# Attention scores of a two-layer hybrid block: the keys' low parts meet only the queries' high part, on half-height tiles of the array

## The chip, the cores and the metric

The kernel runs on one core of one Trainium2 chip. The metric is the device time of one execution in microseconds (us); lower is better. TensorE is called PE, its weight loads PEld, VectorE DVE, ScalarE ACT, GpSimd POOL, and SyncE, which issues most transfers, SP.

## The reference, cut to what matters

Two layers, each with three mixers side by side (an RG-LRU, an SSD scan and a differential attention), an output projection and a SwiGLU network. The change is in the scores of the attention. There are 4 heads, each with two components of 64 features; 1024 latent tokens read 1280 keys (256 context, 1024 latent), and in the first layer the 256 context tokens read the 256 context keys.

```python
def diff_attn_core(q, k, v, lam):
    s = jnp.einsum("bqhcd,bkhcd->bhcqk", q, k).astype(F32)   # c: the two components, d: 64 features
    p = jax.nn.softmax(s, axis=-1)
    w = (p[:, :, 0] - lam * p[:, :, 1]).astype(v.dtype)
    return jnp.einsum("bhqk,bkhd->bqhd", w, v)
```

## The kernel before, in words

Operands of the large products are held as two numbers in a faster matmul type (fp32r): a high part, which is the rounded value, and a low part, which is what rounding took away. A product is then a sum of a few products of parts.

In the attention the 64 features of a component fill only half of the array's 128 rows. The kernel before fills both halves: the tile `qs` holds the queries' high part on rows 0 to 63 and their low part on rows 64 to 127, and the tiles `kh` and `kl` hold the keys' high and low part twice, once on each half. A matmul of `qs` with `kh` gives both products with the keys' high part at once, and one with `kl` both products with the keys' low part, so all four products of parts are formed.

The function `prep(hd)` makes these tiles for a head: `load` brings the raw rows twice, `split_k` and `split_q` make the parts (the rounding copies on ACT, the subtractions on DVE for head 0 and on POOL for the other heads). Its steps are called one at a time, at the place marked "X" in the order of operations, while the head before is worked on.

The work on scores goes in units: one head and 128 queries, 32 latent units in each layer and 4 context units in layer 0. One pass of the loop over `s` (called a step here) does, for units of different age, the operations that the list `K["ops"]` names: "Q0" and "Q1" form the scores of the two components of a unit (the function `qk`; one component of a latent unit is called a part here), "T0" and "T1" transpose the weights of an older unit on PE (`trans`), "P0" and "P1" multiply an older pair of units with the values (`pv`), "E1" is a matmul with ones for a norm (`subln`), "W" and "C" scale and combine the two softmaxes (`weigh` on POOL, `combine` on DVE). A part's scores lie in a PSUM tile `s` of 1280 columns, three banks, of which there are two (`sps`). After the matmuls of a part DVE takes the row maxima (`m`), ACT takes the exponential (`p`), and then the PSUM tile is free for the part after the next.

The order on each engine is set by a scheduler when the kernel is built; in some stages PE follows the order in which the code is written.

Elsewhere the kernel has matmuls that use only some of the array's columns at a time, side by side: L418 (4 tiles of 128 rows by 32 columns, the modulation) and L1064 (2 tiles of 128 rows by 64 columns, in the SSD mixer).

The line numbers below are those of the kernel before: L1212 and L1213 are the score matmuls with `kh` and `kl`, L1216 the maxima, L1220 the exponential, L1249 the transposes, L1259 the products with the values, L1275 the matmul with ones, L1235 the combination, L1172 and L1173 the two operations of `split_q`, L139 and L140 those of `split`.

Of the kernel before, what the change touches and what calls it, by code (L numbers as in the profile page):

```python
# [8 lines left out]
F32 = mybir.dt.float32  # L9
F32R = mybir.dt.float32r  # L10
AF = mybir.ActivationFunctionType
ALU = mybir.AluOpType
AX = mybir.AxisListType

P = 128
# [4 lines left out]
T = NCX + NLAT  # L20
# [56 lines left out]
def kernel(ctx: ExitStack, tc: tile.TileContext, I, out):  # L77
# [3 lines left out]
    act = nc.scalar  # L81
    pool = nc.gpsimd
    pe = nc.tensor
# [7 lines left out]
    def nm(s):  # L91
        uid[0] += 1
        return f"{s}{uid[0]}"
# [17 lines left out]
    def bank(shape, tag="b"):  # L111
        if TAGS[0] is not None:
            tag = "D" if tag == "b" else tag
            return PS[0].tile(shape, F32, tag=tag, name=nm(tag), bufs=TAGS[0][tag])
        return PS[0].tile(shape, F32, tag="b", name=nm("b"))
# [11 lines left out]
    def lagged(f, key=None):  # L127
        if LAG[0] is None:
            return f()
        flush()  # L130
        LAG[0].append((f, key))
# [6 lines left out]
    def split(hi, lo, src, lo_eng=None, key=None):  # L138
        act.copy(hi, src)  # L139
        lagged(lambda: (lo_eng or dve).tensor_tensor(lo, src, hi.bitcast(F32), ALU.subtract), key)  # L140
# [593 lines left out]
    for l in range(DEPTH):  # L734
# [404 lines left out]
        def att(shape, tag, bufs=1, dt=F32, pl=None):  # L1139
            return (pl or AT[1]).tile(shape, dt, tag=tag, name=nm(tag), bufs=bufs)  # L1140
# [4 lines left out]
        def prep(hd):  # L1145

            q0 = NCX if last else 0

            eng = dve if hd == 0 else pool
            pl = AT[hd % 2]  # L1150
            D = HD[hd] = {}

            def load(c, isq):
                t0 = q0 if isq else 0
                raw = D[c, isq] = att([P, T], "raw", 2, F32, at0)
                src = (qD if isq else kD)[hd][64 * c:64 * c + 64, t0:T]
                sy.dma_start(raw[0:64, t0:T], src)
                sy.dma_start(raw[64:128, t0:T], src)

            def first():  # L1160
                for n in ("kh", "kl", "qs"):
                    D[n] = att([P, 2, T], n, 1, F32R, pl)
                load(0, False)
                load(1, False)

            def split_k(c):
                split(D["kh"][:, c, :], D["kl"][:, c, :], D[c, False], eng)
                load(c, True)

            def split_q(c):  # L1170
                raw, qs = D[c, True][:, q0:T], D["qs"][:, c, q0:T]
                act.copy(qs, raw)  # L1172
                eng.tensor_tensor(qs[64:128], raw[64:128], qs[64:128].bitcast(F32), ALU.subtract)  # L1173

            def load_v():
                D["vt"] = att([P, 10, P], "v", 1, F32, pl)
                sy.dma_start(D["vt"], vD[:, hd * P:(hd + 1) * P].rearrange("(j p) d -> p j d", p=P))

            return [first, lambda: split_k(0), lambda: split_k(1), lambda: split_q(0), lambda: split_q(1), load_v]

        units = []
# [6 lines left out]
        def nkey(qb):  # L1188
            return NCX if qb == 0 else T

        def qk(i, c, extra=None):


            hd, qb, qt = units[i]
            D = HD[hd]
            nk = nkey(qb)
            if c == 0:
                U[i] = dict(m=att([P, 4], "m", 3), l=att([P, 4], "l", 3), p=[])
            u = U[i]
            if qb == 0:  # L1200
                if c == 1:
                    return
                parts = [(t, cc, t * P) for t in range(2) for cc in range(2)]
            else:
                parts = [(qt, c, qb * 256 + qt * P)]
            n = len(parts)
            st = sps.tile([P, 1536], F32, tag="s", name=nm("s"))
            s = st[:, 0:n * nk].rearrange("p (n k) -> p n k", n=n)
            for a, (_, cc, tq) in enumerate(parts):
                for k0 in range(0, nk, 512):  # L1210
                    w = min(512, nk - k0)
                    pe.matmul(s[:, a, k0:k0 + w], D["qs"][:, cc, tq:tq + P], D["kh"][:, cc, k0:k0 + w], start=True, stop=False)  # L1212
                    pe.matmul(s[:, a, k0:k0 + w], D["qs"][:, cc, tq:tq + P], D["kl"][:, cc, k0:k0 + w], start=False, stop=True)  # L1213
            if extra is not None:
                extra(st[:, 1280:1536])
            dve.tensor_reduce(u["m"][:, c:c + n], s, AX.X, ALU.max, negate=True)  # L1216
            pt_ = {cc: att([P, n // 2 * nk if n > 1 else nk], *(("p1", 3) if cc else ("p0", 4))) for cc in {cc for _, cc, _ in parts}}
            for a, (_, cc, _) in enumerate(parts):
                p = pt_[cc][:, a // 2 * nk:(a // 2 + 1) * nk]
                act.activation(p, s[:, a, :], AF.Exp, bias=u["m"][:, c + a:c + a + 1], accum_out=u["l"][:, c + a:c + a + 1])  # L1220
                u["p"].append(p)
# [30 lines left out]
        def pv(i, part):  # L1252
            hd, qb, _ = units[i]
            nch = nkey(qb) // P
            if part == 0:
                HD["o", hd, qb] = bank([P, 256])
            op = HD["o", hd, qb]
            for j in range(nch // 2 * part, nch // 2 * (part + 1)):
                pe.matmul(op, HD[hd]["vt"][:, j, :], HD["w", hd, qb][:, j, :], start=(j == 0), stop=(j == nch - 1))  # L1259
            if part == 1:  # L1260
                o = att([P, 256], "o", 3)
                dve.tensor_copy(o, op)
                HD["o", hd, qb] = o

        def subln(i, part):
            hd, qb, _ = units[i]
            o = HD["o", hd, qb]
            if part == 0:
                sq = att([P, 256], "sq", 2)
                pool.tensor_tensor(sq, o, o, ALU.mult)  # L1270
                HD["s", hd, qb] = sq
                return
            if part == 1:
                sp_ = bank([P, 256])
                pe.matmul(sp_, ones, HD["s", hd, qb], start=True, stop=True)  # L1275
                rs = att([P, 256], "rs", 2)
                act.activation(rs, sp_, AF.Ln, scale=1.0 / P, bias=epsc)
                act.activation(rs, rs, AF.Exp, scale=-0.5)
                HD["r", hd, qb] = rs
                return  # L1280
            rs = HD["r", hd, qb]
            dve.scalar_tensor_tensor(o, o, par[l]["gs"], rs, ALU.mult, ALU.mult)
            sy.dma_start(mixD[4 + hd][:, qb * 256:(qb + 1) * 256], o)
# [29 lines left out]
        for s in range(nu + 7):  # L1313
            if s < nu and s % per == 0 and units[s][0] < 3:
                todo = prep(units[s][0] + 1)
            e0 = (lambda ps=None: trans(s - 3, 2, ps)) if isu(s - 3) and units[s - 3][1] else None
            for op in K["ops"][l]:
                if op == "L0" and second(s - 5): subln(s - 5, 0)
                if op == "T0" and isu(s - 3): trans(s - 3, 0)
                if op == "T1" and isu(s - 3): trans(s - 3, 1)  # L1320
                if op == "W" and isu(s - 1): weigh(s - 1)
                if op == "Q0" and isu(s): qk(s, 0, e0)
                if op == "Q1" and isu(s): qk(s, 1)
                if op == "C" and isu(s - 2): combine(s - 2)
                if op == "P0" and second(s - 4): pv(s - 4, 0)
                if op == "P1" and second(s - 4): pv(s - 4, 1)
                if op == "E0" and e0 and not isu(s): e0()
                if op == "E1" and second(s - 5): subln(s - 5, 1)
                if op == "L2" and second(s - 6): subln(s - 6, 2)
                if op == "X" and todo: todo.pop(0)()  # L1330
                if op in ("X", "Q1") and s < 3:
                    for _ in range(2):
                        adaln_step(ada1, None, True)
            if s == 2:
                adaln_end()
# [335 lines left out]
        for d in range(0, KD, 2):  # L1671
            for b in ob:
                s0, n = BLK[b]
# [166 lines left out]
```

## Time and profile before

| | us |
|---|---|
| median of 3 runs | 3141.62 (3140.46 to 3142.94) |
| the profiled execution, its own time | 3142.72 |
| span of the profiled execution, first to last instruction | 3140.7 |
| PE busy in the span | 3013.6 (96%) |
| DVE busy in the span | 2034.3 (65%) |
| ACT busy in the span | 1377.5 (44%) |
| POOL busy in the span | 385.2 (12%) |

The engines work at the same time, so these do not add up. The score matmuls of the attention run from 468.7 to 688 us (layer 0) and from 2106 to 2304 us (layer 1) of the span. A matmul's row in the trace gives its start and a duration that runs to the end of its results; matmuls that follow one another overlap, so how long a matmul holds the array is read from the start of one row to the start of the next.

### The profile page before, as it was taken

What the parts mean: (1) busy time and instruction counts of PE and PEld (TensorE: products, weight loads), DVE (VectorE), ACT (ScalarE), POOL (GpSimd) and SP (SyncE); (2) the same over time, 40 slices, a digit from 0 to 9 for tenths busy, and PEclk for the clock granted to TensorE, in tenths of its full rate; (3) what the DMA queues carried; (4) which work ended last, traced back from release to release, by engine and by line L of the source; (5) the groups of instructions that cost most, each with busy time, mean ns of one, the idle gap of its engine ahead of it and who ended that gap; (6) DMA issues with size and microseconds to landing.
All of it is one profiled execution on the core that took longest, in us unless ns stands there. A gap on an engine that the chain in (4) does not pass through costs nothing. (4 is left out here: it accounts for less than half of the span.)

```text
span 3140.7 us, 41892 instructions
## 1 busy us (share of the span) xinstructions
PE 3013.6 (96%) x15825; PEld 2469.6 (79%) x15825; DVE 2034.3 (65%) x3088; ACT 1377.5 (44%) x2491; POOL 385.2 (12%) x386
## 2 busy tenths in 40 slices
PE   6999998999999999999999899999989899999998
PEld 4888776788778788888888689877868688887887
DVE  5744657976764455557777764668956766666777
ACT  6643736765432323332212645746744433333122
POOL 1113114532000000000000013115421000000000
PEclk8999999999999999999999999999999999999999
DMA  9127565208234331225222224444124122225231
GB/s 310 55 78 216 172 180 140 70 14 265 73 110 134 109 123 59 82 70 200 84 81 84 83 81 126 120 132 131 36 101 150 54 81 81 82 85 195 95 94 61
DMA packets 327441, 353.11 MB, mean 112 GB/s; under 512 B 22237, under 2 KB 269382, under 8 KB 327238
## 3 DMA queue, kind: packets, MB, share of 16 engines
q1 hardware_dynamic: 327062, 350.36, 35.9%
q8 instruction: 124, 2.03, 0.3%
q14 instruction: 79, 0.65, 0.1%
q10 hardware_dynamic: 176, 0.07, 0.0%
HBM read 268.05 MB, written 82.31 MB: 112 GB/s over the span
## 5 line engine op out<-in xcount | busy, mean ns | idle before, releaser
L139 ACT CAST wo<-wr 128x512 fp32r<-128x512 f32 x374 | 230.3, 620 | 451.9 <-issue 145.2
L1467 PE MATMUL A<-x,wo 128*128 128x512 f32 x1584 | 392.4, 396 | 7.2 <-DVE wo L140 5.1
L1659 DVE SCALAR_TENSOR_TENSOR h<-b,mod,h 128x512 f32<-128x512 f32 (+1 forms) x456 | 300.9, 677 | 121.6 <-PE b L123 111.4
L140 DVE TENSOR_TENSOR wo<-wr,wo 128x512 fp32r<-128x512 f32 x374 | 253.8, 688 | 191.9 <-ACT wo L139 186.5
L1467 PEld LDWEIGHTS A<-x,wo 128*128 128x128 f32 x1584 | 294.5, 189 | 81.7 <-issue 7.6
L122 PE MATMUL b<-hl,wo 128*128 128x512 f32 (+1 forms) x912 | 333.8, 366 | 3.2 <-DVE hl L140 3.1
L121 PE MATMUL b<-hh,wo 128*128 128x512 f32 (+1 forms) x912 | 333.3, 366 | 3.6 <-ACT hh L139 3.4
L123 PE MATMUL b<-hh,wo 128*128 128x512 f32 (+1 forms) x912 | 332.4, 365 | 0.0
L121 PE MATMUL b<-xh,wh 128*128 128x512 f32 (+1 forms) x848 | 310.8, 367 | 4.0 <-ACT xh L139 4.0
L122 PE MATMUL b<-xl,wh 128*128 128x512 f32 (+1 forms) x848 | 305.4, 360 | 5.4 <-DVE xl L493 4.2
L123 PE MATMUL b<-xh,wl 128*128 128x512 f32 (+1 forms) x848 | 305.2, 360 | 0.0
L1467 PE MATMUL B<-x,wo 128*128 128x512 f32 x1056 | 263.7, 396 | 8.0 <-DVE x L140 5.5
L1467 PEld LDWEIGHTS B<-x,wo 128*128 128x128 f32 x1056 | 196.9, 189 | 57.4 <-DVE x L140 10.9
L1220 ACT ACTIVATE p<-s,m 128x1280 f32<-128x1280 f32 (+1 forms) x144 | 177.4, 1234 | 69.8 <-DVE m L1216 65.1
L121 PEld LDWEIGHTS b<-hh,wo 128*128 128x128 f32 x912 | 171.7, 189 | 35.7 <-ACT hh L139 4.9
L122 PEld LDWEIGHTS b<-hl,wo 128*128 128x128 f32 x912 | 172.4, 189 | 34.7 <-DVE hl L140 4.9
L1216 DVE TENSOR_REDUCE m<-s 128x1 f32<-128x1280 f32 (+1 forms) x132 | 190.6, 1472 | 10.8 <-PE s L1213 10.7
L123 PEld LDWEIGHTS b<-hh,wo 128*128 128x128 f32 x912 | 172.3, 189 | 28.6
L121 PEld LDWEIGHTS b<-xh,wh 128*128 128x128 f32 x848 | 163.0, 192 | 35.1 <-issue 5.5
L122 PEld LDWEIGHTS b<-xl,wh 128*128 128x128 f32 x848 | 161.7, 191 | 33.0 <-DVE xl L493 4.7
L1212 PE MATMUL s<-kh,qs 128*128 128x512 f32 (+1 forms) x400 | 157.0, 394 | 24.8 <-ACT p L1220 22.0
L123 PEld LDWEIGHTS b<-xh,wl 128*128 128x128 f32 x848 | 161.6, 191 | 23.2
(340 smaller groups left out, 5984.6 us busy)
## 6 DMA issues: line engine op xcount, KB each, us to landing
aw<-in_w_mod_dram SPq DMA_DIRECT2D x96, 512.0 KB, 4.7
wr<-in_w_in_dram SPq DMA_DIRECT2D x44, 512.0 KB, 3.9
wr<-in_w_gate_dram SPq DMA_DIRECT2D x44, 512.0 KB, 3.8
wr<-in_w_up_dram SPq DMA_DIRECT2D x44, 512.0 KB, 3.8
hid<-s SPq DMA_DIRECT2D x44, 512.0 KB, 2.6
wr<-in_w_down_dram SPq DMA_DIRECT2D x44, 512.0 KB, 3.2
t<-hid SPq DMA_DIRECT2D x88, 256.0 KB, 3.1
wr<-in_w_out_dram SPq DMA_DIRECT2D x40, 512.0 KB, 4.4
```

The costliest lines, as they stand in the source:

```text
L121: pe.matmul(o, wh, xh, start=first, stop=False)
L122: pe.matmul(o, wh, xl, start=False, stop=False)
L123: pe.matmul(o, wl, xh, start=False, stop=last)
L139: act.copy(hi, src)
L140: lagged(lambda: (lo_eng or dve).tensor_tensor(lo, src, hi.bitcast(F32), ALU.subtract), key)
L1212: pe.matmul(s[:, a, k0:k0 + w], D["qs"][:, cc, tq:tq + P], D["kh"][:, cc, k0:k0 + w], start=True, stop=False)
L1216: dve.tensor_reduce(u["m"][:, c:c + n], s, AX.X, ALU.max, negate=True)
L1220: act.activation(p, s[:, a, :], AF.Exp, bias=u["m"][:, c + a:c + a + 1], accum_out=u["l"][:, c + a:c + a + 1])
L1467: pe.matmul(o, w[x][:, k, :], r[y][:, k, :], start=first and k == 0 and i == 0, stop=k == 3 and i == 2, skip_group_check=True)
L1659: dve.scalar_tensor_tensor(hv, ps, sect(l, 5, b, d), hv, ALU.mult, ALU.add)
```

## The change

The product of the low parts (keys' low with queries' low) is no longer formed. The keys' low parts are kept once, not twice: keys 0 to 511 and 1024 to 1279 on rows 0 to 63 of a new tile `lq`, keys 512 to 1023 on its rows 64 to 127, beside a copy of the queries' high part for those rows. A part's scores are now three matmuls with `kh` over all 128 rows and then three matmuls with low parts on tiles of 64 rows: 512 keys on the upper half of the array, 512 on the lower half, 256 on the upper half. `split_k` has three subtractions over 64 rows in place of one over 128, `split_q` one more copy on ACT. To make room, three small buffers become fewer (`o` 3 to 2, `sq` and `rs` 2 to 1).

```diff
             def split_k(c):
-                split(D["kh"][:, c, :], D["kl"][:, c, :], D[c, False], eng)
+                raw, kh, lq = D[c, False], D["kh"][:, c, :], D["lq"][:, c, :]
+                act.copy(kh, raw)
+                for r, o, k0, n in ((0, 0, 0, 512), (0, 512, 1024, 256), (64, T, 512, 512)):
+                    r = slice(r, r + 64)
+                    eng.tensor_tensor(lq[r, o:o + n], raw[r, k0:k0 + n], kh[r, k0:k0 + n].bitcast(F32), ALU.subtract)
                 load(c, True)
 
             def split_q(c):
                 raw, qs = D[c, True][:, q0:T], D["qs"][:, c, q0:T]
                 act.copy(qs, raw)
+                act.copy(D["lq"][64:128, c, q0:T], raw[64:128])
                 eng.tensor_tensor(qs[64:128], raw[64:128], qs[64:128].bitcast(F32), ALU.subtract)
...
             for a, (_, cc, tq) in enumerate(parts):
+                q, lq = D["qs"][:, cc, tq:tq + P], D["lq"][:, cc, :]
                 for k0 in range(0, nk, 512):
                     w = min(512, nk - k0)
-                    pe.matmul(s[:, a, k0:k0 + w], D["qs"][:, cc, tq:tq + P], D["kh"][:, cc, k0:k0 + w], start=True, stop=False)
-                    pe.matmul(s[:, a, k0:k0 + w], D["qs"][:, cc, tq:tq + P], D["kl"][:, cc, k0:k0 + w], start=False, stop=True)
+                    pe.matmul(s[:, a, k0:k0 + w], q, D["kh"][:, cc, k0:k0 + w], start=True, stop=False)
+                pe.matmul(s[:, a, 0:min(512, nk)], q[0:64], lq[0:64, 0:min(512, nk)], start=False, stop=True, tile_position=(0, 0))
+                if nk == T:
+                    pe.matmul(s[:, a, 512:1024], lq[64:128, tq:tq + P], lq[64:128, T:T + 512], start=False, stop=True, tile_position=(64, 0))
+                    pe.matmul(s[:, a, 1024:T], q[0:64], lq[0:64, 512:768], start=False, stop=True, tile_position=(0, 0))
```

On PE, in the middle of layer 0's attention, one part (the scores `s`), the transposes after it (`b`, `s` out of `ident` and `p`) stood like this before:

```order
L1212 MATMUL s_4977<-kh_4372,qs_4374 128x512
L1213 MATMUL s_4977<-kl_4373,qs_4374 128x512
L1212 MATMUL s_4977<-kh_4372,qs_4374 128x512
L1213 MATMUL s_4977<-kl_4373,qs_4374 128x512
L1212 MATMUL s_4977<-kh_4372,qs_4374 128x256
L1213 MATMUL s_4977<-kl_4373,qs_4374 128x256
L1249 MATMUL s_4977<-ident,p_4836 128x128 x2
```

and stand like this now (lines of the changed kernel: L1218 is the matmul with `kh`, L1219, L1221 and L1222 are those on half-height tiles, L1258 the transposes, L1268 the products with the values, L1284 the matmul with ones):

```order
L1218 MATMUL s_4989<-kh_4372,qs_4373 128x512 x2
L1218 MATMUL s_4989<-kh_4372,qs_4373 128x256
L1219 MATMUL s_4989<-lq_4374,qs_4373 128x512
L1221 MATMUL s_4989<-lq_4374 128x512
L1222 MATMUL s_4989<-lq_4374,qs_4373 128x256
L1258 MATMUL s_4989<-ident,p_4847 128x128 x2
```

The six matmuls of a part stay together, but the three on half-height tiles now stand between full-height ones. In the whole order there are 153 such runs of half-height matmuls: 119 are the whole three of a part, 16 the single matmul of a context part, and 18 belong to 9 parts whose three are split by other work. Behind 65 of the 153 a transpose follows, behind 88 another full matmul (the products with the values, the matmul with ones, the next part or the modulation).

On PE a context unit (four parts of 256 keys) of layer 0 stands like this now, where before L1212 and L1213 took turns at the same place:

```order
L1218 MATMUL s_5038<-kh_4372,qs_4373 128x256
L1219 MATMUL s_5038<-lq_4374,qs_4373 128x256
L1218 MATMUL s_5038<-kh_4372,qs_4373 128x256
L1219 MATMUL s_5038<-lq_4374,qs_4373 128x256
L1218 MATMUL s_5038<-kh_4372,qs_4373 128x256
L1219 MATMUL s_5038<-lq_4374,qs_4373 128x256
L1218 MATMUL s_5038<-kh_4372,qs_4373 128x256
L1219 MATMUL s_5038<-lq_4374,qs_4373 128x256
```

Here full-height and half-height matmuls alternate one by one, four times in each of four units.

On ACT, in layer 1, where a later head is prepared, the queries' copy `lq` is new among the copies of weights (`wT`) and the exponentials (ACTIVATE):

```order
L1176 CAST qs_18533<-raw_18645 128x1024
L1259 COPY wT_18668<-b_18712 128x4x128
L1177 CAST lq_18534<-raw_18645 64x1024
L1229 ACTIVATE p_18710,l_18676<-s_18702,m_18675 128x1280
L1259 COPY wT_18668<-b_18733 128x4x128
```

Before, the exponential followed the copy of the weights without L1177; there are 16 such casts in the program, 4 of them ahead of the attention's loops.

## Rows read from the trace of the kernel before

**Rows 1.** The page: busy time, share of the span, instructions.

```profile
PE 3013.6 (96%) x15825; PEld 2469.6 (79%) x15825; DVE 2034.3 (65%) x3088; ACT 1377.5 (44%) x2491; POOL 385.2 (12%) x386
```

**Rows 2.** Busy time by stretch, ramp and steady part of each attention; after it clock, DMA.

```profile
core 0: us, PE busy (x) PEld busy (x) DVE busy (x) ACT busy (x) POOL busy (x), PEclk, DMA share, GB/s
468.00:500.00 32.00, 22.12 (x134) 14.09 (x132) 23.78 (x27) 18.31 (x22) 14.28 (x7) 0.89 0.79 213
...
520.00:688.00 168.00, 161.60 (x895) 135.81 (x894) 149.56 (x172) 125.69 (x224) 78.60 (x56) 1.00 0.18 46
...
2150.00:2304.00 154.00, 151.12 (x845) 129.89 (x844) 138.62 (x155) 114.44 (x188) 69.30 (x48) 1.00 0.18 48
```

**Rows 3.** Waits, 2150 to 2300 us: who, for whom, total, times, longest.

```profile
ACT p L1220 <- DVE m L1216: 16.3, 19, 1.4
...
PEld s L1212 <- ACT p L1220: 4.1, 6, 1.4
PE s L1212 <- ACT p L1220: 2.8, 4, 1.1
```

**Rows 4.** PE in order of time, layer 1 attention: start, length, engine, line, operation.

```profile
2227.68 2.32 PE L1259 MATMUL b<-wT,v 128*128 128x256 f32 x10
2229.84 0.60 PE L1249 MATMUL b<-ident,p 128*128 128x128 f32 x4
2230.20 0.48 PE L1212 MATMUL s<-kh,qs 128*128 128x512 f32 x1
2230.52 0.40 PE L1213 MATMUL s<-kl,qs 128*128 128x512 f32 x1
2230.75 0.40 PE L1212 MATMUL s<-kh,qs 128*128 128x512 f32 x1
...
2231.33 0.28 PE L1213 MATMUL s<-kl,qs 128*128 128x256 f32 x1
2231.45 0.38 PE L1249 MATMUL s<-ident,p 128*128 128x128 f32 x2
...
2233.36 2.32 PE L1259 MATMUL b<-wT,v 128*128 128x256 f32 x10
```

**Rows 5.** PE in order of time, SSD mixer of layer 0, around column tiles.

```profile
319.96 0.28 PE L122 MATMUL b<-xl,wh 128*128 128x256 f32 x1
320.08 0.28 PE L123 MATMUL b<-xh,wl 128*128 128x256 f32 x1
320.29 0.64 PE L418 MATMUL ada<-aw,cst 128*32 128x256 f32 x8
...
321.35 0.39 PE L1064 MATMUL b<-E,xt 128*64 128x128 f32 x4
321.57 0.39 PE L1064 MATMUL b<-CE,He 128*64 128x128 f32 x4
321.89 0.51 PE L1036 MATMUL b<-amh,gtr 128*128 128x512 f32 x1
322.23 0.39 PE L1037 MATMUL b<-aml,gtr 128*128 128x512 f32 x1
```

**Rows 6.** PE in order of time, column tiles between score matmuls, layer 0.

```profile
493.98 0.39 PE L1212 MATMUL s<-kh,qs 128*128 128x512 f32 x1
494.21 0.39 PE L1213 MATMUL s<-kl,qs 128*128 128x512 f32 x1
494.53 0.64 PE L418 MATMUL b<-aw,cst 128*32 128x256 f32 x8
495.10 0.39 PE L1212 MATMUL s<-kh,qs 128*128 128x256 f32 x1
495.32 0.28 PE L1213 MATMUL s<-kl,qs 128*128 128x256 f32 x1
```

**Rows 7.** Casts of `split_q` and subtractions for `kl`: durations ns min/median/max.

```profile
L1172 ACT CAST qs<-raw x16: 1034/1150/1263, 463.3 to 2232.0; 128x1280 fp32r<-128x1280 f32 x8, 128x1024 fp32r<-128x1024 f32 x8
...
L140 POOL TENSOR_TENSOR kl<-raw,kh x12: 2890/2928/2959, 479.2 to 2224.5; 128x1280 fp32r<-128x1280 f32 x12
```

More of the change, by code (lines that the diff above doesn't have):

```diff
@@ L1160, in first @@
             def first():
-                for n in ("kh", "kl", "qs"):
-                    D[n] = att([P, 2, T], n, 1, F32R, pl)
+                for n, w in (("kh", T), ("qs", T), ("lq", T + 512)):
+                    D[n] = att([P, 2, w], n, 1, F32R, pl)
                 load(0, False)
@@ L1260, in pv @@
             if part == 1:
-                o = att([P, 256], "o", 3)
+                o = att([P, 256], "o", 2)
                 dve.tensor_copy(o, op)
@@ L1268, in subln @@
             if part == 0:
-                sq = att([P, 256], "sq", 2)
+                sq = att([P, 256], "sq", 1)
                 pool.tensor_tensor(sq, o, o, ALU.mult)
@@ L1275, in subln @@
                 pe.matmul(sp_, ones, HD["s", hd, qb], start=True, stop=True)
-                rs = att([P, 256], "rs", 2)
+                rs = att([P, 256], "rs", 1)
                 act.activation(rs, sp_, AF.Ln, scale=1.0 / P, bias=epsc)
```

## The prediction

> **What bounds the kernel now.** I read the page first. PE is busy for 96% of the span, the next engine, DVE, for 65% [rows 1]. But the change lies in the two attentions alone, so the busy time by stretch counts. It shows a ramp, in which PE is idle for a third of the time (22.12 of 32 us busy), and two long steady parts, in which PE is busy for 161.60 of 168 us and for 151.12 of 154, with DVE at 149.56 and 138.62, that is 89 and 90% [rows 2]. The clock is the full one there (1.00). So in the steady parts PE is the bound with DVE close behind, and PE's idle time in both together is 6.4 + 2.9 = 9.3 us. The waits say the same: what PE still waits for in its score matmuls is the exponential that frees a score tile, 4.1 + 2.8 us in 150, while the exponential waits for the maxima, 16.3 us [rows 3].
>
> The rows in order of time show one step that is bound by PE alone: from the products with the values at 2227.68 to the next at 2233.36, 5.68 us without a wait. In it the reader sees what a matmul holds the array for: 512 score columns 0.23 us (2230.52 to 2230.75), 256 columns 0.12 (2231.33 to 2231.45). The 0.32 of the first one is no extra cost: its row begins while the four transposes ahead are still in the array, and from 2229.84 to 2230.52 the 0.68 us are four transposes of 0.11 and one matmul of 0.23 [rows 4]. So the loads of weights are hidden between full-height matmuls, also where the kind of matmul changes.
>
> **What is saved.** A part held the array for 4 x 0.23 + 2 x 0.12 = 1.16 us [rows 4]. Now it has as many matmuls, of the same lengths; but two of 512 columns lie on different halves and may run side by side. If they do wholly, a part saves 0.23 us. The nearest rows for that are the column tiles: two halves of L1064, four records of 128 columns, take 0.22 us together (321.35 to 321.57), and the eight records of L418, of 256 columns each, take 0.57 (494.53 to 495.10), where one after the other they would need at least 8 x 0.12 [rows 5, 6]. Those tiles plainly overlap. I take the same for row tiles: 119 whole parts x 0.23 = 27.4 us, and in 7 of the split parts 256 columns beside 512, 7 x 0.12 = 0.8. In all 28.2 us of PE's time. The context units save nothing, since they have no pair.
>
> **What is added on PE.** The change puts half-height matmuls between full-height ones, 153 times by the order. What it costs to go from the whole array to tiles and back is in the trace of before, for column tiles:
> - Going in: L123 follows L122 after 0.12 us, L418 follows L123 after 0.21: 0.09 more [rows 5]. Between score matmuls, 0.23 and then 0.32: again 0.09 [rows 6].
> - Coming back: the last L1064 group begins at 321.57 and needs 0.22; the next full matmul begins at 321.89, 0.10 late [rows 5].
> - The first full matmul after it holds the array for 0.34 in place of 0.23 [rows 5], and one of 256 columns for 0.22 in place of 0.12 [rows 6]. That is 0.10 to 0.11 us for a load of 128 columns of weights, which elsewhere lies under the matmul ahead.
>
> A half-height tile also loads 128 columns, so I charge 0.11 for its first load too. The loads of the second and third matmul of a run I charge at nothing: they have the first one's 0.23 us as a cover. A run thus costs 0.09 + 0.11 + 0.10 = 0.30, and what follows it 0.11 more where it is a matmul of 256 or 512 columns. Where a transpose follows (it lasts 0.11, as long as a load), I take half, 0.05. Sum: 153 x 0.30 = 45.9, 88 x 0.11 = 9.7, 65 x 0.05 = 3.3, together 58.9 us. Less the 28.2 saved, PE has 30.7 us more to do.
>
> This charges row tiles at the price of column tiles. No row shows a change of height; the bounds are nothing (the rivals) and the full 0.41.
>
> The Trainium skill (TensorEngine Tiling (Array Packing), Key Properties) says that a change of the tiling mode, unlike a move to another tile of the same mode, drains TensorE; it gives no price and makes no difference between rows and columns. The trace agrees for columns (0.09 and 0.10 us), and no run here shows it for rows; by that rule the first rival below falls.
>
> The Trainium skill (TensorE: Matmul & The Clock Gate, Part 3) reports four row tiles side by side at 3.07 times one. With the same shortfall for two tiles, an estimate from that page, the pair would hold the array for 0.30 us, the saving would be 119 x 0.16 = 19 us, and the time about 8 us above mine; no row here shows it.
>
> **What else is added.** ACT has 16 casts more, 12 of them within the loops, of 1.03 to 1.26 us by the casts of the same width [rows 7]: some 14 us. ACT is busy for 125.69 of 168 and 114.44 of 154 us [rows 2], and it is its exponential that PE waits for; behind a cast stand a copy of weights and an exponential. I take nothing, since a PE that is slower waits less for ACT, and keep 14 us as the upper bound. POOL's subtractions (2.93 us each now) become three of as many columns in all [rows 7]; POOL is busy for less than half of these stretches [rows 2], and the parts are needed a head later: nothing. On DVE the same happens for head 0, ahead of the loops. The smaller buffers hold values that are used up within two steps: nothing.
>
> **What of it shows.** PE's 9.3 us of waits in the steady parts are steps in which DVE or ACT is late; there a longer part fills a wait. I take half of them, 4.7 us, as filled. In the ramps a part's scores are a link in the chain scores, maxima, exponential, free tile, so they count whole. The sum, against the profiled execution's own time: 3142.7 + 30.7 - 4.7 = 3168.7 us. That execution lies 1.1 us above the median of the runs, so the forecast is **3167.6 us**, 0.8% slower. Its own range: at the low end no cost ahead of transposes (-3.3) and all waits filled (-4.6), 3159.7, and a little for the ramps, 3158; at the high end no wait filled (+4.7) and the casts in the way (+14), 3186.
>
> **The rivals.**
> - *The change of height costs nothing.* Half-height tiles are then just two more places for weights, loads go ahead as before, and PE has 28.2 us less to do. For it: nothing in the trace shows that a change of rows behaves as one of columns. Against it: the changes of both kinds that the rows show cost the same 0.09 to 0.10, whether the tiles have 32 columns or 64 [rows 5, 6]. DVE then decides: of the 154 us, about 50 parts x 0.23 = 11.5 go, PE would need 140, and DVE has 138.6 and its own waits. I give two thirds of the saving, 19 us: 3141.6 - 19 = 3123 us. This side wins as soon as a run costs less than 28.2 / 153 = 0.18 us; the rows say 0.30 plus the load behind it.
> - *Only the emptying costs, the loads are hidden* (0.09 + 0.10 a run, 29.1 us, against 28.2 saved): 3142 or 3143 us, no change. For it: a load into one half might be made while the other half works. Against it: ahead of a run and behind it the whole array works.
> - *The change doesn't do what it says:* the two halves run one after the other, the 28.2 us aren't saved, and the time is 3167.6 + 28.2 = 3196 us. For it: both write all 128 partitions of PSUM, which the column tiles don't. Against it: they write different banks, the column tiles overlap.
>
> **How the numbers follow.** The forecast 0.57, the free change 0.19, the hidden loads 0.13, no overlap 0.11. A measurement of this kernel tells about 0.2% (6 us) from no change. Faster by more than that is the free change and a sliver of the third, 0.20; slower is the forecast and the last, 0.68; 0.12 remain for no change. The range leaves out the last rival and the edges: 3120 to 3186; the likeliest case's own is 3158 to 3186.
>
> **What would show it.** In the trace after: the two rows of 512 columns on different halves start within a few hundredths (overlap right) or 0.23 apart (wrong); the row of the first half-height matmul starts 0.09 later than its forerunner's 0.12; from it to the next full-height one 0.11 + 0.35 + 0.10 = 0.56 pass; the first full matmul after it holds 0.34 or 0.22. A step of two latent parts grows from 5.68 to about 6.0 us, and PE's waits for the exponential shrink. If the first half-height row follows after 0.12 and the next full-height one after 0.35, the price is wrong and the first rival holds. If steps grow while PE waits more for ACT's exponential, the casts were mispriced.

## The result

The changed kernel takes 3169.44 us (median of 4 runs, 3165.34 to 3176.34); before is 3141.98 us with the runs beside it. The ratio is 1.009, with a 95% interval of 1.0077 to 1.0102: 27 us slower. A second set of 5 runs, below, gave 3172.07 us against 3142.21, with nearly the same ratio (1.0089). The forecast was 3167.6 us. The profiled execution is the slowest of its runs, 3176.34 us, so its rows add up to 33.8 us and not to 27.

First the stretches that answer to [rows 2], of the changed kernel (its attentions begin 2 and 26 us later, so the stretches are shifted and, in the two steady ones, longer: us, then busy time of PE, PEld, DVE, ACT, POOL, the clock, the transfers):

```profile
468.00:520.00 52.00, 45.37 (x205) 27.14 (x203) 32.07 (x38) 33.85 (x41) 19.91 (x14) 0.67 0.69 185
```

```profile
524.00:711.00 187.00, 179.53 (x907) 131.38 (x905) 151.91 (x175) 132.51 (x229) 82.53 (x65) 0.98 0.16 44
2176.00:2338.00 162.00, 156.71 (x828) 119.29 (x828) 132.18 (x153) 116.90 (x189) 69.68 (x55) 0.97 0.16 43
```

PE is still the engine that is busy nearly always; DVE's share fell from 89 and 90% to 81 and 82, because the steps are longer and its work is the same. PE is idle for 7.5 + 5.3 = 12.8 us in 349, where it was 9.3 in 322. The granted clock is 0.98 and 0.97 here, where it was 1.00 [rows 2]: some of this time PE ran at the lower of its two levels, 1.2 GHz in place of 2.4. The account at the end comes back to that.

The rows that answer to [rows 4], PE in order of time in the changed kernel's second attention (start, length, engine, line, operation):

```profile
2226.20 0.82 PE L1218 MATMUL s<-kh,qs 128*128 128x512 f32 x3
2226.95 0.49 PE L1219 MATMUL s<-lq,qs 64*128 64x512 f32 x1
2226.95 0.49 PE L1221 MATMUL s<-lq 64*128 64x512 f32 x1
2227.29 0.28 PE L1222 MATMUL s<-lq,qs 64*128 64x256 f32 x1
2227.49 0.44 PE L1258 MATMUL s<-ident,p 128*128 128x128 f32 x2
2227.77 0.60 PE L1258 MATMUL b<-ident,p 128*128 128x128 f32 x4
2228.12 0.83 PE L1218 MATMUL s<-kh,qs 128*128 128x512 f32 x3
2228.88 0.49 PE L1219 MATMUL s<-lq,qs 64*128 64x512 f32 x1
2228.88 0.50 PE L1221 MATMUL s<-lq 64*128 64x512 f32 x1
2229.22 0.28 PE L1222 MATMUL s<-lq,qs 64*128 64x256 f32 x1
2229.42 0.70 PE L1284 MATMUL b<-sq,ones 128*128 128x256 f32 x2
2229.96 2.32 PE L1268 MATMUL b<-wT,v 128*128 128x256 f32 x10
```

Here the reader sees, at the full clock, what the change does on PE. The two matmuls of 512 columns on different halves start together (2226.95 and 2226.95): they overlap wholly. The third begins 0.34 later, which is 0.23 for the pair and 0.11 for a first load that nothing covers; then 0.20 pass for 256 columns that need 0.12, up to the next full-height matmul (2227.29 to 2227.49). A run lasts 0.54, with 0.56 forecast. A part, from its first matmul to what follows, takes 1.29 to 1.30 us, where it took 1.25 [rows 4]; and a full matmul behind it takes longer: the two records of the matmul with ones 0.54 (2229.42 to 2229.96), where they took 0.43 before. The prediction's step from 5.68 to about 6.0 us did not come: the next two steps take 5.74 and, with the matmul with ones, 6.39 us (2229.96 to 2235.70 and to 2242.09), together 12.13. In the kernel before, such pairs that nothing holds up take 11.63 to 11.69. That is 0.11 to 0.12 a part, where the forecast's step means 0.16.

### The profile page after: what moved, and what is told of

Same layout as the page of the kernel before. It is cut to its first block, busy times and chain, and to the rows that moved or that the text cites. A ratio compares the mean times of both kernels' runs of the same rounds, so it can differ in the third digit from the quotient of the medians.

```text
span 3174.5 us, 41940 instructions
## 1 busy us (share of the span) xinstructions
PE 3056.5 (96%) x15825; PEld 2461.1 (78%) x15825; DVE 2030.0 (64%) x3096; ACT 1396.8 (44%) x2507; POOL 392.3 (12%) x410
## 5 line engine op out<-in xcount | busy, mean ns | idle before, releaser
L1268 PE MATMUL b<-wT,v 128*128 128x256 f32 x656 | 157.1, 385 | 1.3 <-ACT wT L1259 1.3
```

## The experiments

**All low parts on one half.** The overlap alone is taken away; the runs of half-height matmuls stay.

```diff
-for r, o, k0, n in ((0, 0, 0, 512), (0, 512, 1024, 256), (64, T, 512, 512)):
+for r, o, k0, n in ((0, 0, 0, 512), (0, 512, 512, 512), (0, 1024, 1024, 256)):
...
+for k0 in range(0, nk, 512):
+    w = min(512, nk - k0)
+    pe.matmul(s[:, a, k0:k0 + w], q[0:64], lq[0:64, k0:k0 + w], start=False, stop=True, tile_position=(0, 0))
```

> All of the keys' low parts on the upper half: three half-height matmuls of 512, 512 and 256 columns a part, one after the other; as many runs of half-height matmuls (153) as the changed kernel has. Theory A (a run costs 0.3 us and an uncovered load, and the two halves overlap wholly, which saves 0.23 us a part): 119 x 0.23 = 27 us more than the changed kernel, about 3196 us. Rival B (the overlap is worth nothing; the loss is in waits for ACT and the clock): 3169 us, as the changed kernel.

Measured: 3193.55 us, ratio 1.0166 (1.0150 to 1.0181), 24 us above the changed kernel. PE in order of time:

```profile
2240.58 0.82 PE L1218 MATMUL s<-kh,qs 128*128 128x512 f32 x3
2241.34 0.85 PE L1221 MATMUL s<-lq,qs 64*128 64x512 f32 x3
2242.11 0.44 PE L1257 MATMUL s<-ident,p 128*128 128x128 f32 x2
```

A part takes 1.53 us (2240.58 to 2242.11), 0.24 more than with both halves. So the overlap is real and worth what it was charged, against rival B. Of what the clock takes this run says nothing.

**Two runs a part.** The same matmuls, the overlap kept, but with a full-height matmul between the pair and the third low one.

```diff
-for k0 in range(0, nk, 512):
+for k0 in range(0, nk, 512)[:2]:
...
     pe.matmul(s[:, a, 512:1024], lq[64:128, tq:tq + P], lq[64:128, T:T + 512], start=False, stop=True, tile_position=(64, 0))
+    pe.matmul(s[:, a, 1024:T], q, D["kh"][:, cc, 1024:T], start=True, stop=False)
     pe.matmul(s[:, a, 1024:T], q[0:64], lq[0:64, 512:768], start=False, stop=True, tile_position=(0, 0))
```

> The changed kernel with the third high matmul between the pair and the third low matmul, so that a part has two runs of half-height matmuls, 279 in all in place of 153; the work is the same. Theory A: 126 more runs at 0.09 + 0.11 + 0.10 + 0.11 = 0.41 us are 52 us, some of it in waits: 3205 to 3222 us. Rival B (runs are cheap, the loss is elsewhere): 3165 to 3180 us.

Measured: 3206.32 us, ratio 1.0204 (1.0190 to 1.0217), 37 us above the changed kernel. PE in order of time:

```profile
2241.86 0.71 PE L1218 MATMUL s<-kh,qs 128*128 128x512 f32 x2
2242.50 0.49 PE L1219 MATMUL s<-lq,qs 64*128 64x512 f32 x1
2242.50 0.49 PE L1221 MATMUL s<-lq 64*128 64x512 f32 x1
2242.92 0.39 PE L1222 MATMUL s<-kh,qs 128*128 128x256 f32 x1
2243.24 0.38 PE L1223 MATMUL s<-lq,qs 64*128 64x256 f32 x1
2243.55 0.44 PE L1259 MATMUL s<-ident,p 128*128 128x128 f32 x2
```

A part takes 1.69 us (2241.86 to 2243.55): 0.40 more for one more run, with 0.41 expected. A full-height matmul of 256 columns between two runs holds the array for 0.32 (2242.92 to 2243.24) in place of 0.12. The total grew by 37 and not by the 50 that 126 x 0.40 makes, since PE's waits for the exponential shrank: in its score matmuls, over both attentions, from 8.8 + 12.8 to 5.0 + 3.4 us. The clock helped too: it is 1.00 in the steady stretches (522.21 to 708.75 us and 2195.44 to 2370.10), where the changed kernel has 0.98 and 0.97. The price of a run put between full-height matmuls is shown, and the total lies just inside what was expected.

**Full height, the new order and the small buffers.** The kernel before with the high matmuls first, then the low ones, and with the smaller `o`, `sq` and `rs`; no half-height run.

```diff
-    pe.matmul(s[:, a, k0:k0 + w], D["qs"][:, cc, tq:tq + P], D["kl"][:, cc, k0:k0 + w], start=False, stop=True)
+for k0 in range(0, nk, 512):
+    w = min(512, nk - k0)
+    pe.matmul(s[:, a, k0:k0 + w], D["qs"][:, cc, tq:tq + P], D["kl"][:, cc, k0:k0 + w], start=False, stop=True)
...
-o = att([P, 256], "o", 3)
+o = att([P, 256], "o", 2)
```

> The kernel before (all four products, full height) with two things of the change alone: the three matmuls with the high parts first and then the three with the low parts, and the smaller buffers o, sq, rs. No half-height run. Theory A: within 0.2% of before, 3136 to 3148 us. Rival C (the order of the matmuls or the smaller buffers cost it): 3155 us or more.

Measured: 3143.09 us, ratio 1.0004 (0.9995 to 1.0013). PE in order of time:

```profile
2230.90 0.83 PE L1212 MATMUL s<-kh,qs 128*128 128x512 f32 x3
2231.57 0.74 PE L1215 MATMUL s<-kl,qs 128*128 128x512 f32 x3
2232.15 0.38 PE L1251 MATMUL s<-ident,p 128*128 128x128 f32 x2
```

Neither the order nor the buffers cost anything; rival C falls. The rows also give the entry's price directly: three high matmuls and on to the low ones take 0.67 here (2230.90 to 2231.57), and 0.76 where the low ones are of half height (2228.12 to 2228.88), 0.09 more. The low ones take 0.58 here and 0.54 there: overlap and uncovered cost nearly cancel within the run, and what is paid is the entry and the load behind the run.

**The queries' copy on POOL.**

```diff
-act.copy(D["lq"][64:128, c, q0:T], raw[64:128])
+eng.tensor_copy(D["lq"][64:128, c, q0:T], raw[64:128])
```

> The changed kernel with the queries' copy for the lower half made on POOL (DVE for head 0) in place of ACT; 150 runs. Theory A: PE's own work is unchanged, only PE's waits for the exponential behind the copies go (some 8 us more of them in layer 1 than before): 3160 to 3169 us. Rival B (the copies ahead of the exponentials are the loss): at most 3150 us.

Measured: 3167.85 us, ratio 1.0085 (1.0071 to 1.0099), not distinguishable from the changed kernel. ACT's casts are not the bulk of the loss.

**The changed kernel once more.** No edit.

> The changed kernel once more, for a second profile and beside the three below. Profile of it so far: 41 and 20 us at the half clock (0.50) within the two attentions, where before has 10 and 10. Theory A: 3165 to 3172 us whatever that share is. Rival D (the half clock at the attentions' beginnings is a good part of the loss): the time follows the share at the half clock, the copy-on-POOL run with 31 and 7 us having been the fastest.

Measured: 3172.07 us, ratio 1.0089 (1.0076 to 1.0103), the upper end of what theory A expected. The stretch from 468 to 520 us again has a low clock:

```profile
468.00:520.00 52.00, 45.36 (x205) 27.11 (x203) 32.08 (x38) 32.77 (x41) 19.97 (x14) 0.67 0.68 178
```

This does not rule out rival D. In the profiled executions the time goes with the time at 1.2 GHz in the two attentions: 41 + 20 us of it and 3176.34 us in the first profile, 38 + 17 and 3172.39 in this one, 31 + 7 and 3167.04 with the copies on POOL, though that kernel has another edit too. The four runs of the first set point the same way: the slowest, 3176.34 us, has a mean granted clock of 0.974, the fastest, 3165.34 us, one of 0.980.

**Full height in the first five units.** The first five units of each attention have full-height matmuls only.

```diff
+if i < 5:
+    for k0 in range(0, nk, 512):
+        w = min(512, nk - k0)
+        pe.matmul(s[:, a, k0:k0 + w], q, D["kh"][:, cc, k0:k0 + w], start=False, stop=True)
+    continue
```

> The changed kernel with full-height matmuls in the first five units of each attention, where the product with the low parts is left out and the one with the high parts is done twice in its place (the timing pattern of the kernel before; the scores of these units are not the reference's). 131 runs of half-height matmuls in place of 153. Theory A alone: 22 x 0.38 - 20 x 0.23 = 4 us less, some of it in waits: 3164 to 3168 us. Rival D (half-height matmuls in the ramp bring the half clock, and that costs): the half clock in the first attention falls from 30 to 40 us to about 10, and the time to 3160 us or less.

Measured: 3166.52 us, ratio 1.0076 (1.0063 to 1.0089), 5.5 us below the 3172.07 us of the changed kernel; the intervals overlap. The same stretch:

```profile
468.00:520.00 52.00, 42.61 (x220) 29.25 (x219) 34.24 (x40) 33.72 (x44) 22.51 (x15) 0.80 0.75 195
```

The clock rose from 0.67 to 0.80, not to the kernel before's 0.90, and 24 us at 1.2 GHz are left in the first attention, not the 10 that rival D asks for; so this run tests it only in part. The total lies where theory A put it, but not for its reason alone: in the profiles this kernel's first score matmul comes 2.5 us earlier (468.59, and 471.08 in the profile above), a lead that it has before the edited code begins, and the way from the first row maximum to the thirteenth is 2.7 us shorter (44.4 and 47.1). What of that the runs give and what the clock can't be told apart.

**PE in program order.** Both attentions' PE is held to the order in which the code is written, which keeps a part's three half-height matmuls together.

```diff
-    "cp": 22565 | 64 | 128,
+    "cp": 22565 | 64 | 128 | 16 | 1024,
```

> The changed kernel with PE in program order within both attentions, so that the three half-height matmuls of a part are never split: 144 runs in place of 153. Theory A: 9 x 0.38 = 3 us less for the runs, against what the fixed order costs in waits, which no run shows yet: 3160 to 3185 us. It is the control of the next one.

Measured: 3199.4 us, ratio 1.0179 (1.0165 to 1.0193), worse than the upper end expected. The fixed order costs some 27 us against 3172.07, far more than nine runs are worth.

**Both parts of a unit in one run.** As the last, with one run a unit.

```diff
-    "ops": [["P0", "T0", "Q0", "T1",
+    "ops": [["P0", "T0", "T1", "Q0",
...
+for cc, st in enumerate(sts):
+    for k0, w in ((0, 512), (512, 512), (1024, 256)):
+        pe.matmul(st[:, k0:k0 + w], D["qs"][:, cc, tq:tq + P], D["kh"][:, cc, k0:k0 + w], start=True, stop=False)
+for cc, st in enumerate(sts):
+    q, lq = D["qs"][:, cc, tq:tq + P], D["lq"][:, cc, :]
+    pe.matmul(st[:, 0:512], q[0:64], lq[0:64, 0:512], start=False, stop=True, tile_position=(0, 0))
...
```

> As the ordered one, with the two parts of a unit together: both with the high parts at full height first, then both with the low parts in one run; the transposes of an older unit stand ahead of both. 80 runs in place of 144, the same matmuls. Theory A: 64 x (0.09 + 0.11 + 0.10 + about 0.08) = 24 us less than the ordered one on PE, against later maxima of the first part: 3140 to 3165 us. A rival (runs are cheap): as the ordered one or slower.

Measured: 3343.74 us, ratio 1.0638 (1.0624 to 1.0653): far outside what was expected. PE in order of time:

```profile
2271.52 0.85 PE L1218 MATMUL s<-kh,qs 128*128 128x512 f32 x3 [0.66 <-ACT p L1229]
2272.83 0.85 PE L1218 MATMUL s<-kh,qs 128*128 128x512 f32 x3 [0.46 <-ACT p L1229]
2273.61 0.49 PE L1221 MATMUL s<-lq,qs 64*128 64x512 f32 x1
2273.61 0.49 PE L1222 MATMUL s<-lq 64*128 64x512 f32 x1
2273.95 0.28 PE L1223 MATMUL s<-lq,qs 64*128 64x256 f32 x1
2273.95 0.39 PE L1222 MATMUL s<-lq 64*128 64x512 f32 x1
```

The run itself does what it should: the second part's lower matmul starts beside the first part's third (2273.95 both). But both score tiles are now needed at once, so PE waits for the exponential ahead of each part, and by the order in which it is written the first part's low matmuls, and with them its maxima, come only after the second part's high matmuls. For the price of a run this one says nothing; it shows that merging runs across parts does not pay in this order with two score tiles.

## Why the prediction was right, point by point

**PE as the bound of the steady parts: right.** PE is busy for 96 and 97% of the longer stretches, what lengthens PE's work alone lengthens the time (24 us with one half, 37 with two runs a part), and ACT's casts, the new order and the small buffers, tried apart from the rest, change it by no more than the measurement can tell.

**The saving, 0.23 us a part by overlap: right.** The pair starts together, and with one half only a part takes 0.24 more. The estimate from the Trainium skill (TensorE: Matmul & The Clock Gate, Part 3), 0.30 for the pair, did not come true here: two tiles of 64 rows, 0.23 us, lost nothing against one.

**The price of a run at that of column tiles: right in its pieces, too high in the sum.** Entry 0.09 (0.09 measured); the first load 0.11 (0.34 less 0.23); the return 0.10 (0.20 less 0.12, so 0.08 to 0.09); the load behind it 0.11 for a matmul of 256 columns (0.54 for two records, less 0.43 [rows 4, ten of them in 2.16]) and 0.05 for transposes (0.28 for two, less 0.22: 0.06). The rule that the Trainium skill has in TensorEngine Tiling (Array Packing), Key Properties, that a change of the mode drains the engine, agrees with these rows for heights too, with 0.09 us to go in. The rival that a change of height costs nothing is out, and so is the one in which the loads are hidden.

With the measured pieces the sum is 119 whole parts at 0.11 (50, transposes behind) or 0.16 (69) = 16.5 us, 16 context runs at about 0.38 = 6 us, and 9 split parts at about 0.66 = 6 us: some 28 us, where the forecast had 30.7. But the time does not show that much. It is seen in two stretches that hold as many matmuls in both kernels (848, and 834 or 835): from the thirteenth row maximum of the first attention to the 65th, and from the thirteenth of the second to its last (first the two of the kernel before, then the same two of the changed one):

```profile
518.18:678.62 160.44, 154.04 (x848) 129.13 (x848) 142.71 (x165) 118.73 (x212) 77.09 (x54) 1.00 0.19 50
2152.10:2304.68 152.58, 149.71 (x835) 128.58 (x834) 137.20 (x154) 112.69 (x185) 67.64 (x47) 1.00 0.17 47
```

```profile
524.16:699.70 175.54, 168.07 (x848) 122.80 (x848) 143.07 (x165) 124.82 (x216) 79.22 (x62) 0.98 0.17 46
2175.93:2339.27 163.34, 158.05 (x834) 120.13 (x833) 133.52 (x154) 117.45 (x189) 70.03 (x55) 0.97 0.16 43
```

The two are 25.9 us longer: PE is idle for 3.5 us more (12.8 and 9.3) and busy for 22.4 more. Of the 22.4, some 7 to 8 belong to the clock, as is shown below. The 14 to 15 us that remain, an estimate, are what 117 of the 153 runs cost less what the overlap saved; at the forecast's rate they would be 30.7 x 117 / 153 = 23.5. The second profile of the changed kernel gives the same: 18.6 us more busy, some 3 of them by the clock. One reason can be read: where transposes follow, the six of them up to the next part take 0.63 us (2227.49 to 2228.12) and took 0.57 to 0.66 before (2225.43 to 2226.00, 2231.45 to 2232.11), so little of the load behind the run comes on top there. Which runs make the rest of the difference was not separated.

**The waits: wrong.** The forecast let a slower PE fill half of its 9.3 us of waits, -4.7. They grew instead, to 12.8 us in steady stretches that are 8% longer. The page of waits names the place, from 2165 to 2338 us in the changed kernel:

```profile
PE s L1218 <- ACT p L1229: 5.3, 2, 3.3
ACT qs L1176 <- DMA raw<-q: 4.7, 2, 3.0
```

Two waits for the exponential, of which one is 3.3 us; in the kernel before the longest is 1.1 [rows 3]. They are where the next head is prepared. ACT in order of time:

```profile
2246.83 0.59 ACT L1259 COPY wT<-b 128x512 f32<-128x512 f32 x1 [0.94 <-PE b L1258]
2250.45 1.04 ACT L1176 CAST qs<-raw 128x1024 fp32r<-128x1024 f32 x1 [3.04 <-DMA raw<-q]
2251.51 1.04 ACT L1177 CAST lq<-raw 64x1024 fp32r<-64x1024 f32 x1
2252.58 1.33 ACT L1229 ACTIVATE p<-s,m 128x1280 f32<-128x1280 f32 x1
```

The cast stands ahead of the exponential on ACT and waits for the raw queries; those are loaded into a buffer that POOL must first have read, and POOL's three subtractions take longer there than one did:

```profile
2241.32 4.60 POOL L1171 TENSOR_TENSOR lq<-raw,kh 64x512 fp32r<-64x512 f32 x3
```

4.60 us in place of 2.93 [rows 7] for as many columns, and 3.29 ahead of the other wait (from 2188.96). POOL ends at 2245.92, SP issues the load at 2245.95, and the cast begins at 2250.45. So two steps that were costed at nothing, POOL's subtractions and ACT's casts, come into the path at such a place; how much of a wait each of them makes was not tried apart. With the copies on POOL the longest of these waits was 2.2 us and the time the same within the measurement, so it is a few us at most. With two runs a part a still slower PE did fill its waits: 2.5 and 0.7 us of idle time between the same row maxima.

**The clock: put at nothing, and it cost.** The prediction read 1.00 for the steady parts and took that for the changed kernel too. There PE ran at 1.2 GHz three times, for 17 us in all: from 621.6, from 2201.9 and from 2253.1 us. Each came with a wait of PE just before it or across its beginning: 1.0 and 1.6 us, 2.0, and 3.3. The last of them:

```profile
2254.05 1.44 PE L1218 MATMUL s<-kh,qs 128*128 128x512 f32 x3 [3.33 <-ACT p L1229]
2255.41 0.79 PE L1219 MATMUL s<-lq,qs 64*128 64x512 f32 x1
...
2256.35 0.69 PE L1258 MATMUL s<-ident,p 128*128 128x128 f32 x2
```

A part takes 2.30 us here (2254.05 to 2256.35) and 1.30 at the full clock. At that ratio the 16 us in which PE was busy at the lower level cost 7, and at a half 8. In the second profile 7 us at 1.2 GHz are left in these stretches, and a wait of 3.25 us there is not followed by it, so a wait of this length does not always bring it.

**The total: right in part by luck.** Of the profiled execution's 33.8 us, 25.9 lie in the two stretches above: 14 to 15 for the runs, 7 to 8 for the clock, 3.5 for waits. The first attention's ramp, from the first to the thirteenth row maximum, takes 3.6 more. The first attention begins 2.4 us later (first score matmul at 471.11, 468.75 before), a delay that arises long before the edited code, between 50 and 80 us, where the clock is 0.75 and was 0.94 and where both kernels do the same. Some 2 us are spread over the rest. So the price of the runs was put too high, by some 9 us in the two stretches, the waits too low by 8 (+3.5 in place of -4.7), and the clock was left out; one error takes up much of the other two. For the profiled execution they leave 7.6 us (3176.34, and 3168.7 by the prediction's sum); that the median lies within 2 us of the forecast is luck.

## What to carry to other kernels

Before putting a few matmuls on part of the array between full-height ones, count the changes: each visit here cost about 0.4 us (0.09 in, 0.11 for the first load, 0.09 out, up to 0.11 for the load behind), so it needs more than 0.4 us of overlap to pay; a part of 768 low columns saved 0.23. The price could be read in the trace of before from tiles of another kind. And a preparation step that is split into more instructions on an idle engine is not free when the buffer that it reads is what the next load waits for. Last, before calling a sum right, compare stretches with the same instructions: here the total hid two terms that were wrong and one that was missing.

## What was not expected of the hardware

In the ramp of the first attention the granted clock fell: 0.67 from 468 to 520 us in both profiles of the changed kernel, 0.64 with one half, 0.77 with two runs a part and with the copy on POOL, 0.80 with full height in the first five units; without half-height runs it was 0.90, before and with the new order alike. A stretch below 1.00 is one with time at the lower level, 1.2 GHz. PE was busy there for longer in the changed kernel, not shorter (45.37 us of 52, 39.35 before), with fewer matmuls (205 and 226), most of them at 1.2 GHz: from 478 to 512 us the clock is 0.50 throughout. In the ramp itself it cost little: the first to the thirteenth row maximum took 43.5 us before and 47.1 after, of which 12 parts at 0.11 to 0.16 explain 1.3 to 1.9. Why half-height runs go with more time at the lower level is open; the stretch from 50 to 80 us, 0.94 before and 0.75 in both profiles of the changed kernel, shows that the clock also differs where the two kernels do the same.
